# One Strassen step in the gate and up projections of the middle groups of a two-layer decoder trunk

## The chip, the cores and the metric

The kernel runs on one core of a Trainium2 chip. The metric is the device time of one execution in microseconds (us). The engines are named as the profile names them: PE (matrix multiply) and PEld (its weight loads), DVE (vector), ACT (scalar), POOL (GpSimd) and SP, which issues the transfers from HBM.

## What is computed

Two layers; in each a half-step SwiGLU feed-forward block (FFN), a token mixer and a second FFN, with an RMSNorm before and behind each. So there are four FFNs. The change touches the FFNs alone.

```python
D_MODEL = 1024
SEQ = 512
D_FF = 2816
...
def _swiglu(x, wg, wu, wd):
    return (jax.nn.silu(x @ wg) * (x @ wu)) @ wd
...
    for l in range(DEPTH):
        g = norm_g[l]
        h = _swiglu(_rmsnorm(x, g[0]), ffn_w_gate[l, 0], ffn_w_up[l, 0], ffn_w_down[l, 0])
        x = x + 0.5 * _rmsnorm(h, g[1])
```

Inputs and outputs are float32.

## The kernel before

**Numbers.** A float32 operand is held as a pair of tiles in the matmul's 32-bit format, the rounded value (`hi`, written by ACT, `split`, L69) and the rest (`lo`, written by DVE, also L69). A product of two such operands is three matmuls (`mm3`, L74 to L76): hi by hi, hi by lo and lo by hi. The normalized input `hT` of an FFN lies in SBUF as such a pair, channels on the partitions: 8 blocks of 128 channels by 512 tokens.

**The FFN.** The 2816 hidden channels are 22 blocks f of 128. For one f, the gate and the up projection take one weight unit of 128x1024 each (`unit`, L90: a load of 512 KB into one of three buffers `raw`, then the split into `whi` and `wlo`), and 8 channel blocks times three matmuls of 512 columns each (`proj`), into one PSUM bank each. `evac` (L208) turns the two banks into the activations: ACT takes silu of the gate, DVE multiplies by the up projection, and the product is split into `ahi` and `alo`.

Two f make a group g; there are 11 groups. `down(g)` multiplies the activations of a group by the two units of the down matrix: the first 512 output columns gather in four PSUM banks `acc` (24 matmuls), the second 512 go through the four banks `mm` (24 matmuls) and DVE adds each of these banks to a tile `ysb` in SBUF (L252). Group 0 has a form of its own (`first_projs`, matmuls of 256 columns, token half by token half, while the input is still being transposed), and so has group 10, at the end. In between the program is `gate_up(g)` and then `down(g - 1)`, for g = 1 to 9.

**Order.** Each engine works through its own list of instructions in order. The lists are made when the program is built: a scheduler places the instructions, and each instruction carries the semaphore waits that its operands ask for. PSUM holds four rotating banks `mm` and four `acc`. SP issues one load after the other; a load waits until its `raw` buffer is free.

Of the kernel before, what the change touches and what calls it, by code (L numbers as in the profile page):

```python
# [40 lines left out]
class Kernel:  # L41
# [41 lines left out]
    def unit(self, src, inner, pool=None, eng=None):  # L83
# [8 lines left out]
        return [z.rearrange("p (k c) -> p k c", c=inner) for z in (hi, lo)]  # L92

    def proj(self, out, u, toks=slice(0, S), m=P):

        for k in range(KD):
            last = self.mm3(out, [z[:, k, :m] for z in u], [z[:, k, toks] for z in self.hT], k == 0, k == KD - 1)
        return last
# [5 lines left out]

    def first_projs(self, srcs, pooled=3, pool=None):

        units = []
        for n, s in enumerate(srcs):
            units.append(self.unit(s, P, pool, self.nc.gpsimd if n < pooled else None))
            if self.begin:  # L110
                self.guard = self.turned
# [85 lines left out]
    def ffn(self, l, s, norms, nxt, held=None):  # L197
        nc, tc, a = self.nc, self.tc, self.a
        wg, wu, wd = (a[w][l, s] for w in ("ffn_w_gate", "ffn_w_up", "ffn_w_down"))
        with ExitStack() as ctx:  # L200
            self.ring = self.pool("ring", 6, ctx)
            dring = self.pool("dring", 4, ctx, side="right" if l % 2 and s else "left")
            act, yp = self.pool("act", 6, ctx), self.pool("yp", 1, ctx)
            gains = self.pool("gains", 1, ctx)
            ysb = [yp.tile([P, 512], F32, name=f"ysb{t}") for t in range(NT)]
# [12 lines left out]
            def gate_up(g):  # L218
                fs = (2 * g, 2 * g + 1)
                if g == 0:  # L220
                    pg0, pu0, pg1, pu1 = self.first_projs([wg[0], wu[0], wg[1], wu[1]],
                                                          0 if held else 3, dring if s else None)
                    evac(0, pg0, pu0)
                    evac(1, pg1, pu1)
                    return
                for f in fs:
                    evac(f, self.proj_new(wg[f]), self.proj_new(wu[f]))

# [39 lines left out]
            last = [(f, self.unit(wg[f], P), self.unit(wu[f], P)) for f in (NF - 2, NF - 1)]  # L268
            load_down(ng - 2)
# [678 lines left out]
```

## Time and profile before

| | |
|---|---|
| time, median of 3 runs (range) | 1953.24 us (1952.72 to 1953.73) |
| profiled execution: its own time | 1956.74 us |
| profiled execution: its span, first to last instruction | 1955.0 us |
| granted TensorE clock, mean over the span | 0.993 of full speed |
| PE busy | 1918.8 us (98%) |
| PEld, DVE, ACT, POOL busy | 83%, 48%, 37%, 9% |

The span is what the profile's rows add up to; the execution's own time is 1.7 us more. The profiled execution lies 3.5 us (0.2%) over the median of the timed runs.

### The profile page before, as it was taken

Reading aid. Unit: us, or ns where it says so; the run is one execution under the profiler, and the core shown is the slowest. Engines: PE = TensorE matmul, PEld = TensorE weight load, DVE = VectorE, ACT = ScalarE, POOL = GpSimd, SP = SyncE. Lnnn points to the kernel's source line nnn. Section 1 sums busy time; section 2 is a strip of 40 time slices with the busy share of each in tenths; the row PEclk is TensorE's granted clock in tenths of the full one; section 3 lists DMA queues with packets and bytes.
Section 4 is the critical chain, followed back from the end, with each engine's and each line's share of the span. In section 5 each row is a group of like instructions: output and inputs, shape, how many; then the busy total and the mean of one; then the engine's idle time right before and its main releaser. Section 6 shows DMA issues by size and latency. Waiting matters only on the chain.

```text
span 1955.0 us, 24019 instructions
## 1 busy us (share of the span) xinstructions
PE 1918.8 (98%) x9715; PEld 1631.1 (83%) x9715; DVE 939.9 (48%) x1356; ACT 722.6 (37%) x1244; POOL 185.6 (9%) x250
## 2 busy tenths in 40 slices
PE   9999999999999999999999999999999989999998
PEld 8888888987788888888988888898888888888887
DVE  5333333589665333333634343356667563333333
ACT  6322221434764222222532222236666553222221
POOL 1000000332230000000200000014331210000000
PEclk9999999999999999999999999999999999999999
DMA  5423232131034232321342323222212323232311
GB/s 193 130 86 108 86 129 75 45 99 65 22 98 150 85 101 92 102 91 49 120 139 86 108 86 108 65 77 66 65 55 65 108 76 129 87 107 87 107 54 44
DMA packets 51265, 178.39 MB, mean 91 GB/s; under 512 B 7346, under 2 KB 7346, under 8 KB 51154
## 3 DMA queue, kind: packets, MB, share of 16 engines
q1 hardware_dynamic: 51154, 176.86, 28.0%
q8 instruction: 76, 1.25, 0.3%
q14 instruction: 35, 0.29, 0.0%
HBM read 174.74 MB, written 2.10 MB: 90 GB/s over the span
## 4 chain that ended last, share of the span: by engine, by line
PE 52%; issue 39%; DVE 3%; ACT 3%; POOL 2%; DMA 1%; POOLq 0%; DVEq 0%; SPq 0%; ACTq 0%
PE mm L74 14%; PE mm L75 14%; PE mm L76 14%; PE acc L74 2%; PE acc L75 2%; PE acc L76 2%; ACT whi L69 1%; PE mm L708 1%; DVE yv L381 1%; POOL rstd L136 1%; PE mm L718 1%; ACT junk L141 1%; POOL ms L134 1%; DMA raw<-in_ffn_w_up_dram 0%; POOL wlo L69 0%
## 5 line engine op out<-in xcount | busy, mean ns | idle before, releaser
L74 PE MATMUL mm<-hhi,whi 128*128 128x512 f32 (+1 forms) x1952 | 696.1, 359 | 8.7 <-ACT hhi L69 8.3
L75 PE MATMUL mm<-hlo,whi 128*128 128x512 f32 (+1 forms) x1952 | 697.9, 358 | 1.8 <-DVE hlo L69 1.6
L76 PE MATMUL mm<-hhi,wlo 128*128 128x512 f32 (+1 forms) x1952 | 697.3, 358 | 0.0
L69 ACT CAST whi<-raw 128x1024 fp32r<-128x1024 f32 x319 | 330.9, 1050 | 901.0 <-issue 264.0
L69 DVE TENSOR_TENSOR wlo<-raw,whi 128x1024 fp32r<-128x1024 f32 (+1 forms) x293 | 353.9, 1222 | 370.1 <-ACT whi L69 355.8
L74 PEld LDWEIGHTS mm<-hhi,whi 128*128 128x128 f32 x1952 | 370.5, 191 | 63.5 <-ACT hhi L69 10.2
L75 PEld LDWEIGHTS mm<-hlo,whi 128*128 128x128 f32 x1952 | 371.8, 191 | 54.9 <-DVE hlo L69 3.0
L76 PEld LDWEIGHTS mm<-hhi,wlo 128*128 128x128 f32 x1952 | 371.8, 190 | 52.1
L215 DVE TENSOR_TENSOR wk<-mm,wk 128x512 f32<-128x512 f32 (+1 forms) x96 | 62.1, 647 | 290.6 <-PE mm L76 245.2
L252 DVE TENSOR_TENSOR ysb<-mm,ysb 128x512 f32<-128x512 f32 x128 | 88.5, 692 | 161.3 <-PE mm L76 161.3
L134 POOL TENSOR_SCALAR ms<-ss 128x1 f32<-128x1 f32 x48 | 23.6, 491 | 1464.5 <-ACT junk L141 1464.4
L76 PE MATMUL mm<-whi,alo 128*128 128x512 f32 x352 | 137.1, 389 | 0.0
L75 PE MATMUL mm<-wlo,ahi 128*128 128x512 f32 x352 | 137.0, 389 | 0.0
L76 PE MATMUL acc<-whi,alo 128*128 128x512 f32 x352 | 136.9, 389 | 0.0
L74 PE MATMUL acc<-whi,ahi 128*128 128x512 f32 x352 | 136.9, 389 | 0.0
L75 PE MATMUL acc<-wlo,ahi 128*128 128x512 f32 x352 | 136.9, 389 | 0.0
L74 PE MATMUL mm<-whi,ahi 128*128 128x512 f32 x352 | 136.8, 390 | 0.0
L214 ACT ACTIVATE wk<-mm 128x512 f32<-128x512 f32 (+1 forms) x96 | 53.2, 555 | 69.6 <-PE mm L76 69.6
L76 PEld LDWEIGHTS mm<-whi,alo 128*128 128x128 f32 x352 | 66.1, 188 | 13.9
L74 PEld LDWEIGHTS acc<-whi,ahi 128*128 128x128 f32 x352 | 66.1, 188 | 13.8
L76 PEld LDWEIGHTS acc<-whi,alo 128*128 128x128 f32 x352 | 66.0, 188 | 13.8
L75 PEld LDWEIGHTS acc<-wlo,ahi 128*128 128x128 f32 x352 | 66.1, 188 | 13.7
(211 smaller groups left out, 1964.5 us busy)
## 6 DMA issues: line engine op xcount, KB each, us to landing
raw<-in_ffn_w_gate_dram SPq DMA_DIRECT2D x88, 512.0 KB, 3.4
raw<-in_ffn_w_up_dram SPq DMA_DIRECT2D x88, 512.0 KB, 3.9
raw<-in_ffn_w_down_dram SPq DMA_DIRECT2D x88, 512.0 KB, 3.4
raw<-in_fox_w_qk_dram SPq DMA_DIRECT2D x16, 512.0 KB, 3.5
raw<-in_ab_w_in_dram SPq DMA_DIRECT2D x14, 512.0 KB, 3.4
raw<-in_ab_w_out_dram SPq DMA_DIRECT2D x8, 512.0 KB, 3.4
raw<-in_fox_w_out_dram SPq DMA_DIRECT2D x8, 512.0 KB, 3.5
gpost<-in_norm_g_dram SPq DMA_DIRECT2D x6, 512.0 KB, 3.9
```

The lines of the kernel that those rows point to most:

```text
L69: return nc.scalar.copy(hi, src), (eng or nc.vector).tensor_tensor(lo, src, hi.bitcast(F32), ALU.subtract)
L74: mm(out, a[0], b[0], start=start, stop=False)
L75: mm(out, a[0], b[1], start=False, stop=False)
L76: return mm(out, a[1], b[0], start=False, stop=stop)
L134: nc.gpsimd.tensor_scalar(ms, ss[:, 0:1], ss[:, 1:2], eps, ALU.add, ALU.add)
L136: nc.gpsimd.tensor_tensor(r, ms, self.mhalf, ALU.pow)
L141: return self.nc.scalar.activation(junk, src, AF.Square, scale=scale, accum_out=out)
L214: nc.scalar.activation(sg, pg, AF.Silu)
L215: nc.vector.tensor_tensor(av, pu, sg, ALU.mult)
L252: nc.vector.tensor_tensor(ysb[t], p, ysb[t], ALU.add)
L381: nc.vector.scalar_tensor_tensor(yv[c], av[c][:, k : k + S], cw[:, c, k : k + 1], yv[c], ALU.mult, ALU.add)
L708: nc.tensor.transpose(pt[:, c0 : c0 + P], pr[b][:, kb * P : (kb + 1) * P], self.ident)
```

## The change

For f = 2 to 19 (the groups 1 to 9) gate and up are computed together by one Strassen step (in Winograd's form), three matmuls per product as before. The 2x2 blocks of the weight matrix are gate/up by channel halves: `a11`, `a12` are the two channel halves of the gate's unit, `a21`, `a22` those of the up unit (128x512 each). The 2x2 blocks `B` of the input are channel halves by token halves (four blocks of 128 channels by 256 tokens). Seven block products `m1` to `m7`, each four channel blocks times three matmuls of 256 columns, stand for the eight of the plain form: 84 matmuls of 256 columns for 48 of 512. For this

- `combine` makes, once for each FFN, the four sums of input blocks `T[1]` to `T[4]` on DVE, and splits them;
- `winograd(f)` makes four sums of weight blocks on DVE (`s1`, `s2`, and both again), splits seven pieces of 128x512 (`phi`, `plo`) where there were two units of 128x1024, and puts the products together with seven DVE additions of 256 columns out of PSUM, one ACT copy, silu and one multiplication. `m1` and `m5` share a bank, so do `m7` and `m6`, and `m2` and `m3`; the order on PE is m1, m5, m7, m6, m2, m4 and m3.

`down(0)` now stands ahead of `gate_up(1)`; the pools are cut anew (ring 10 halves for 6 units, `act` 4 for 6, the gains' tiles after the sums of the input are given up).

```diff
-            self.ring = self.pool("ring", 6, ctx)
+            self.ring = self.pool("ring", 10, ctx)
...
-                    evac(f, self.proj_new(wg[f]), self.proj_new(wu[f]))
+                    winograd(f)
...
+            halves = slice(0, 256), slice(256, 512)
+            B = {(r, c): [z[:, 4 * r : 4 * r + 4, halves[c]] for z in self.hT] for r in (0, 1) for c in (0, 1)}
+            T = {}
+
+            def combine():
...
+                for ks in (slice(0, 2), slice(2, 4)):
+                    b = {n: [z[:, ks, :].bitcast(F32) for z in w] for n, w in B.items()}
+                    t = {n: self.wk().rearrange("p (k c) -> p k c", c=256) for n in T}
+                    for n, p, m in ((1, (0, 0), (0, 1)), (3, (1, 1), (0, 1))):
+                        v.tensor_tensor(t[n], b[p][0], b[m][0], ALU.subtract)
+                        v.tensor_tensor(t[n], t[n], b[p][1], ALU.add)
+                        v.tensor_tensor(t[n], t[n], b[m][1], ALU.subtract)
+                    for n, p, m in ((2, 1, (1, 1)), (4, 2, (1, 0))):
+                        v.scalar_tensor_tensor(t[n], t[p], -1.0, b[m][0], ALU.mult, ALU.subtract)
+                        v.tensor_tensor(t[n], t[n], b[m][1], ALU.subtract)
+                    for n in (1, 3, 2, 4):
+                        self.split(*[z[:, ks, :] for z in T[n]], t[n])
+
+            def winograd(f):
+                rg, ru = self.load(wg[f]), self.load(wu[f])
+                a11, a12, a21, a22 = (r[:, n * 512 : n * 512 + 512] for r in (rg, ru) for n in range(2))
+                add = lambda o, x, y: nc.vector.tensor_tensor(o, x, y, ALU.add)
+                left, right = halves
+                banks = [self.psum() for _ in range(4)]
+                m1, m7, m2, m4 = (p[:, left] for p in banks)
+                m5, m6, m3 = (p[:, right] for p in banks[:3])
+
+                def product(out, w, b):
+                    for k in range(4):
+                        self.mm3(out, [z[:, k, :] for z in w], [z[:, k, :] for z in b], k == 0, k == 3)
+
+                w1, w2, sg, s1, s2 = (self.wk() for _ in range(5))
+                product(m1, self.piece(a11), B[0, 0])
+                nc.scalar.copy(w1[:, left], m1)
+                add(s1, a21, a22)
+                product(m5, self.piece(s1), T[1])
+                add(s2, s1, a11)
+                add(s1, a11, a21)
+                product(m7, self.piece(s1), T[3])
+                product(m6, self.piece(s2), T[2])
+                add(w1[:, right], m6, w1[:, left])
+                add(w2[:, left], m7, w1[:, right])
+                add(w2[:, right], m5, w2[:, left])
+                add(w1[:, right], m5, w1[:, right])
+                add(s2, s2, a12)
+                product(m2, self.piece(a12), B[1, 0])
+                add(w1[:, left], m2, w1[:, left])
+                product(m3, self.piece(s2), B[1, 1])
+                add(w1[:, right], m3, w1[:, right])
+                nc.scalar.activation(sg, w1, AF.Silu)
+                product(m4, self.piece(a22), T[4])
+                add(w2[:, left], m4, w2[:, left])
+                nc.vector.scalar_tensor_tensor(w2, sg, -1.0, w2, ALU.mult, ALU.mult)
+                aT[f] = [act.tile([P, S], F32R, name=n) for n in ("ahi", "alo")]
+                self.split(*aT[f], w2)
...
-            for g in range(1, ng - 1):
+            combine()
+            down(0, True)
+            gate_up(1)
+            for g in range(2, ng - 1):
                 gate_up(g)
-                down(g - 1, g == 1)
+                down(g - 1, False)
```

Three places of the instruction lists show what this does to the order. In the rows, a name's number is a buffer's; `raw`, `phi`, `plo`, `whi`, `wlo` are as above, and `wk` are work tiles.

**DVE over one middle group, before.** The list from the last addition of a `down` to the last split of the next group's activations (L215 is the multiplication in `evac`):

```order
L252 TENSOR_TENSOR ysb3_202<-mm_1316,ysb3_202 128x512
L69 TENSOR_TENSOR wlo_1675<-raw_1672,whi_1674 128x1024
L69 TENSOR_TENSOR wlo_1681<-raw_1678,whi_1680 128x1024
L69 TENSOR_TENSOR wlo_1606<-raw_1603,whi_1605 128x1024
L215 TENSOR_TENSOR wk_1389<-mm_1355,wk_1388 128x512
L69 TENSOR_TENSOR wlo_1637<-raw_1634,whi_1636 128x1024
L69 TENSOR_TENSOR alo_1387<-wk_1389,ahi_1386 128x512
L69 TENSOR_TENSOR wlo_1744<-raw_1741,whi_1743 128x1024
L215 TENSOR_TENSOR wk_1459<-mm_1425,wk_1458 128x512
L69 TENSOR_TENSOR wlo_1775<-raw_1772,whi_1774 128x1024
L69 TENSOR_TENSOR alo_1457<-wk_1459,ahi_1456 128x512
```

The weight units that are split here are used later: `wlo_1675` and `wlo_1681` are for the `down` of this group.

**First place: DVE and PE behind a `down`, after.** The list of DVE from the last additions of a `down` into the first f of the next group (L335 is the addition to `ysb`, L277 `add`; `wk_1633` is `s1`, `wk_1634` is `s2`):

```order
L335 TENSOR_TENSOR ysb2_198<-mm_1606,ysb2_198 128x512
L69 TENSOR_TENSOR alo_1551<-wk_1420,ahi_1550 128x512
L335 TENSOR_TENSOR ysb3_199<-mm_1614,ysb3_199 128x512
L277 TENSOR_TENSOR wk_1633<-raw_1624 128x512
L277 TENSOR_TENSOR wk_1634<-wk_1633,raw_1622 128x512
L69 TENSOR_TENSOR plo_1654<-wk_1633,phi_1653 128x512
L277 TENSOR_TENSOR wk_1633<-raw_1622,raw_1624 128x512
L69 TENSOR_TENSOR plo_1672<-wk_1633,phi_1671 128x512
L69 TENSOR_TENSOR plo_1688<-wk_1634,phi_1687 128x512
L69 TENSOR_TENSOR plo_1709<-raw_1622,phi_1708 128x512
L277 TENSOR_TENSOR wk_1634<-wk_1634,raw_1622 128x512
```

PE has, behind the last matmul of that `down` (into `mm_1614`), the twelve of m1, whose last three stand here, and then m5 and m7 (`mm_1627`), which read the pieces of `s1`:

```order
L74 MATMUL mm_1626<-hhi_118,phi_1635 128x256
L75 MATMUL mm_1626<-hlo_119,phi_1635 128x256
L76 MATMUL mm_1626<-hhi_118,plo_1636 128x256
L74 MATMUL mm_1626<-t1hi_504,phi_1653 128x256
L75 MATMUL mm_1626<-t1lo_505,phi_1653 128x256
L76 MATMUL mm_1626<-t1hi_504,plo_1654 128x256
```

The piece of `s1` is now made behind the last addition of the `down`, and its first user stands twelve matmuls behind that `down` on PE. On ACT the copy of m1 (L289) stands ahead of the cast `phi_1653`.

**Second place: DVE between the two f of a group, after.** From the addition of m4 of the first f to the first pieces of the second (`wlo_1911` and `wlo_1917` are the units of the down matrix, L308 is the last multiplication of `winograd`):

```order
L277 TENSOR_TENSOR wk_1631<-mm_1629,wk_1631 128x256
L69 TENSOR_TENSOR wlo_1911<-raw_1908,whi_1910 128x1024
L277 TENSOR_TENSOR wk_1630<-mm_1628,wk_1630 128x256
L277 TENSOR_TENSOR wk_1776<-raw_1767 128x512
L308 SCALAR_TENSOR_TENSOR wk_1631<-wk_1632,wk_1631 128x512
L277 TENSOR_TENSOR wk_1777<-wk_1776,raw_1765 128x512
L69 TENSOR_TENSOR plo_1797<-wk_1776,phi_1796 128x512
L69 TENSOR_TENSOR alo_1762<-wk_1631,ahi_1761 128x512
L277 TENSOR_TENSOR wk_1776<-raw_1765,raw_1767 128x512
L69 TENSOR_TENSOR wlo_1917<-raw_1914,whi_1916 128x1024
L69 TENSOR_TENSOR plo_1815<-wk_1776,phi_1814 128x512
```

The load of `raw_1908` waits for the buffer of `raw_1624` (the up unit of the first f), whose last reader is the split of `a22`, `plo_1744`; that of `raw_1914` waits for `wlo_1911`. PE has between m3 of the first f and m5 of the second twelve matmuls of `down`, which read `whi_1910` and `wlo_1911`.

**Third place: DVE at the start of the first FFN.** Before, from the first multiplication of group 0:

```order
L215 TENSOR_TENSOR wk_474<-mm_224,wk_473 128x512
L69 TENSOR_TENSOR wlo_593<-raw_590,whi_592 128x1024
L69 TENSOR_TENSOR wlo_631<-raw_628,whi_630 128x1024
L69 TENSOR_TENSOR alo_472<-wk_474,ahi_471 128x512
L69 TENSOR_TENSOR wlo_637<-raw_634,whi_636 128x1024
L215 TENSOR_TENSOR wk_482<-mm_226,wk_481 128x512
L69 TENSOR_TENSOR wlo_704<-raw_701,whi_703 128x1024
```

And after, from the same multiplication (L231) into the sums of the input (L265 to L270):

```order
L231 TENSOR_TENSOR wk_487<-mm_237,wk_486 128x512
L69 TENSOR_TENSOR alo_485<-wk_487,ahi_484 128x512
L231 TENSOR_TENSOR wk_495<-mm_239,wk_494 128x512
L265 TENSOR_TENSOR wk_512<-hhi_118 128x512
L265 TENSOR_TENSOR wk_513<-hhi_118 128x512
L266 TENSOR_TENSOR wk_512<-wk_512,hlo_119 128x512
L69 TENSOR_TENSOR alo_493<-wk_495,ahi_492 128x512
L266 TENSOR_TENSOR wk_513<-wk_513,hlo_119 128x512
```

The sums stand behind the multiplication that waits for the last bank of group 0 (`mm_239`). From there to the piece of the first `s1` there are 31 instructions of 128x512 on DVE, while PE has the 48 matmuls of `down(0)` and the twelve of the first m1.

## Rows read from the trace of the kernel before

**Rows 1.** The page: busy us and share of the span of each engine

```profile
PE 1918.8 (98%) x9715; PEld 1631.1 (83%) x9715; DVE 939.9 (48%) x1356; ACT 722.6 (37%) x1244; POOL 185.6 (9%) x250
```

**Rows 2.** Busy time by engine in one middle group (windows), with granted clock

```profile
233.33:265.97 32.64, 32.64 (x145) 27.03 (x144) 12.43 (x15) 8.38 (x10) 0.00 (x0) 1.00 0.30 98
```

**Rows 3.** Timeline of DVE in that group: start, us, instruction, idle before

```profile
233.33 0.69 DVE L252 TENSOR_TENSOR ysb<-mm,ysb 128x512 f32<-128x512 f32 x1 [2.93 <-PE mm L76]
...
237.41 0.69 DVE L252 TENSOR_TENSOR ysb<-mm,ysb 128x512 f32<-128x512 f32 x1 [0.67 <-PE mm L76]
238.02 1.22 DVE L69 TENSOR_TENSOR wlo<-raw,whi 128x1024 fp32r<-128x1024 f32 x1
...
249.85 0.69 DVE L215 TENSOR_TENSOR wk<-mm,wk 128x512 f32<-128x512 f32 x1 [3.57 <-PE mm L76]
...
265.97 0.69 DVE L252 TENSOR_TENSOR ysb<-mm,ysb 128x512 f32<-128x512 f32 x1 [2.93 <-PE mm L76]
```

**Rows 4.** Timeline of ACT in that group, the split behind DVE's L215

```profile
250.57 0.62 ACT L69 CAST ahi<-wk 128x512 fp32r<-128x512 f32 x1 [0.28 <-DVE wk L215]
```

**Rows 5.** Timeline, all engines: matmuls of 512 columns, and DVE behind one

```profile
300.90 0.39 PE L76 MATMUL mm<-whi,alo 128*128 128x512 f32 x1
...
301.33 0.69 DVE L252 TENSOR_TENSOR ysb<-mm,ysb 128x512 f32<-128x512 f32 x1 [0.67 <-PE mm L76]
...
303.62 0.39 PE L74 MATMUL mm<-hhi,whi 128*128 128x512 f32 x1
...
304.30 0.39 PE L74 MATMUL mm<-hhi,whi 128*128 128x512 f32 x1
```

**Rows 6.** Timeline of PE in group 0: matmuls of 256 columns

```profile
24.01 0.28 PE L74 MATMUL mm<-hhi,whi 128*128 128x256 f32 x1
...
24.36 0.28 PE L74 MATMUL mm<-hhi,whi 128*128 128x256 f32 x1
```

**Rows 7.** Groups by line and shape: count, busy us, mean ns, idle before

```profile
L69 DVE TENSOR_TENSOR wlo<-raw,whi 128x1024 fp32r<-128x1024 f32 x290 | 351.3, 1225 | 369.0 <-ACT whi L69 354.7 <-PE mm L76 4.7
L69 ACT CAST whi<-raw 128x1024 fp32r<-128x1024 f32 x316 | 328.6, 1052 | 898.6 <-issue 264.0 <-PE mm L76 254.4 <-DMA raw<-in_ffn_w_down_dram 179.8
L69 DVE TENSOR_TENSOR alo<-wk,ahi 128x512 fp32r<-128x512 f32 x80 | 54.8, 685 | 2.7 <-ACT ahi L69 2.7
L69 ACT CAST ahi<-wk 128x512 fp32r<-128x512 f32 x80 | 49.6, 621 | 23.3 <-DVE wk L215 23.3
L156 DVE SCALAR_TENSOR_TENSOR x<-wk,rstd,x 128x512 f32<-128x512 f32 x48 | 33.9, 747 | 3.5 <-POOL rstd L136 3.1
L173 ACT ACTIVATE wk<-wk,rstd 128x512 f32<-128x512 f32 x24 | 17.3, 720 | 10.2 <-POOL rstd L136 9.9
L215 DVE TENSOR_TENSOR wk<-mm,wk 128x256 f32<-128x256 f32 x16 | 6.8, 425 | 44.7 <-ACT wk L214 44.7
L214 ACT ACTIVATE wk<-mm 128x256 f32<-128x256 f32 x16 | 6.1, 381 | 51.5 <-PE mm L76 51.5
```

**Rows 8.** Timeline of DVE at the end of an FFN

```profile
354.57 0.69 DVE L295 TENSOR_TENSOR ysb<-mm,ysb 128x512 f32<-128x512 f32 x1 [4.80 <-PE mm L76]
355.30 0.69 DVE L152 TENSOR_TENSOR wk<-ysb,gpost 128x512 f32<-128x512 f32 x1
```

**Rows 9.** DMA issues: count, KB each, median us from issue to landing

```profile
raw<-in_ffn_w_down_dram SPq DMA_DIRECT2D x88, 512.0 KB, 3.4
```

**Rows 10.** Timeline of PE in a mixer: matmuls behind two waits

```profile
496.76 0.44 PE L472 MATMUL mm<-ident,z 128*128 128x128 f32 x2 [2.77 <-ACT z L464]
...
531.68 0.50 PE L74 MATMUL mm<-whi,chi 128*128 128x512 f32 x1 [1.69 <-ACT chi L69]
532.01 0.40 PE L75 MATMUL mm<-wlo,chi 128*128 128x512 f32 x1
```

**Rows 11.** The same windows view around the first of these waits

```profile
495.00:500.00 5.00, 3.24 (x13) 2.76 (x13) 5.00 (x12) 3.52 (x12) 0.03 (x1) 0.71 0.00 0
```

More of the change, by code (lines that the diff above doesn't have):

```diff
@@ L92, in unit, with piece, pieces @@
         return [z.rearrange("p (k c) -> p k c", c=inner) for z in (hi, lo)]
+    def piece(self, src, eng=None):
+        pair = [self.ring.tile([P, 512], F32R, name=n) for n in ("phi", "plo")]
+        with ExitStack() as after:
+            for ins in self.guard:
+                after.enter_context(self.tc.issue_after(ins.ins))
+            self.split(*pair, src, eng)
+        return [z.rearrange("p (k c) -> p k c", c=P) for z in pair]
+    def pieces(self, src, eng=None):
+        raw = self.loaded.pop(0) if self.loaded else self.load(src)
+        return tuple(self.piece(raw[:, n * 512 : n * 512 + 512], eng) for n in range(2))
     def proj(self, out, u, toks=slice(0, S), m=P):
         for k in range(KD):
-            last = self.mm3(out, [z[:, k, :m] for z in u], [z[:, k, toks] for z in self.hT], k == 0, k == KD - 1)
+            w = [z[:, k % 4, :] for z in u[k // 4]] if isinstance(u, tuple) else [z[:, k, :m] for z in u]
+            last = self.mm3(out, w, [z[:, k, toks] for z in self.hT], k == 0, k == KD - 1)
         return last
@@ L103, in proj_new, with first_projs @@
         return out
-    def first_projs(self, srcs, pooled=3, pool=None):
+    def first_projs(self, srcs, pooled=3, pool=None, pieces=False):
         units = []
         for n, s in enumerate(srcs):
-            units.append(self.unit(s, P, pool, self.nc.gpsimd if n < pooled else None))
+            eng = self.nc.gpsimd if n < pooled else None
+            units.append(self.pieces(s, eng) if pieces else self.unit(s, P, pool, eng))
             if self.begin:
@@ L221, in gate_up @@
                     pg0, pu0, pg1, pu1 = self.first_projs([wg[0], wu[0], wg[1], wu[1]],
-                                                          0 if held else 3, dring if s else None)
+                                                          0 if held else 3, dring, not s)
                     evac(0, pg0, pu0)
@@ L259, in ffn @@
                 held.close()
-            for g in range(1, ng - 1):
+            combine()
+            down(0, True)
+            gate_up(1)
+            for g in range(2, ng - 1):
                 gate_up(g)
-                down(g - 1, g == 1)
+                down(g - 1, False)
+            combos.close()
+            gains = self.pool("gains", 1, ctx)
             with tc.issue_after(self.loading.ins) if held else ExitStack():
@@ L267, in ffn @@
                 gpre = self.load_gain(gains, *nxt, "gpre") if nxt else None
-            last = [(f, self.unit(wg[f], P), self.unit(wu[f], P)) for f in (NF - 2, NF - 1)]
+            last = [(f, self.pieces(wg[f]), self.pieces(wu[f])) for f in (NF - 2, NF - 1)]
             load_down(ng - 2)
```

8 lines of the change are left out of this document (6 added, 2 removed).

## The prediction

> **What bounds the kernel now.** The page comes first: PE is busy for 98% of the span, DVE for 48%, ACT for 37% [rows 1]. A busy PE need not be a PE at its peak, so the next view is the windows of one middle group: PE busy in all 32.64 us of it, at the full clock, DVE in 12.43, ACT in 8.38 [rows 2]. The timeline of DVE then shows the period: the first addition of a `down` comes at 233.33 and 265.97 us, 32.64 us apart [rows 3]. A group is 144 matmuls of 512 columns; 32.64/144 is 0.2267 us each, and three successive ones stand 0.68 us apart on the timeline [rows 5]. So PE never waits in the middle groups: DVE and ACT split weights that are needed later, and the kernel goes as fast as matmuls follow each other. The reader is to see two things here: only fewer or shorter matmuls can help, and the slack of DVE (20 us in a group) is what the change spends.
>
> **What PE saves.** In `first_projs` three matmuls of 256 columns take 0.35 to 0.36 us [rows 6]; I take 0.12 each. Two of them (0.24) cost more than one of 512 (0.2267), so of the eighth that the step saves in columns little over half is left: for one f, 48 x 0.2267 = 10.88 us become 84 x 0.12 = 10.08, a gain of 0.80 us. The eighteen f of an FFN give 14.4 us, the four FFNs 57.6. A group would go from 32.64 to 168 x 0.12 + 48 x 0.2267 = 31.04 us.
> The Trainium skill (TensorE: Matmul & The Clock Gate, Back-to-back issue gap) gives a gap of N/2.4 + 2.5 ns, that is 109 and 216 ns, and by it the gain would be 48 x 0.2158 - 84 x 0.1092 = 1.19 us for one f and 85 us in all. The rows show 120 and 227, so this page is too good for both shapes, and the sum goes by the rows.
>
> **What DVE gets.** For one f DVE had two units of 1.225 us, one multiplication and one split; now it has seven pieces and four weight sums (0.69 each), seven additions of 256 columns (0.425), the last multiplication (0.75) and a split (0.69) [rows 7]. With two down units and four additions, a group comes to 14 x 0.69 + 8 x 0.69 + 14 x 0.425 + 2 x 0.75 + 2 x 0.69 + 2 x 1.225 + 4 x 0.69 = 29.2 us of 31.04. Instructions that don't depend on each other overlap by 0.08 us (237.41 to 238.02 for one of 0.69 us [rows 3]), which brings it near 26. DVE is thus not the bound in sum. But it is now early enough only where its order lets it run ahead, and at four kinds of joint the order does not. The prices for a hand-over: DVE starts 0.43 us after the start of the last matmul it needs (300.90 to 301.33 [rows 5]), that is 0.20 behind PE's issue; an instruction that needs the one before it starts 0.04 after its end [rows 8]; ACT starts 0.03 after DVE (249.85 + 0.69 to 250.57 [rows 3, 4]), and I take as much from ACT to DVE and 0.05 to PE; a cast of 512 takes 0.62, silu from SBUF 0.72 (as L173), a copy of 256 columns out of PSUM 0.38 [rows 7]; the first matmul behind a wait costs PE 0.1 more (0.33 us to the next for 0.23 [rows 10]).
>
> **Joint A, behind a `down` (first place of the change's lists).** Time 0 is where PE has issued the last matmul of the `down`. The last `ysb` addition runs from 0.20 to 0.89, `s1` from 0.81 to 1.50. PE issues m1 until 1.44, ACT copies it from 1.64 to 2.02 and only then casts `s1`, until 2.6; `plo` of `s1` is ready at 3.32. The third matmul of m5 needs it: 3.35 where 1.68 would have been free, 1.7 us lost. `s1` is then overwritten (its reader was that split): 3.35 to 4.04, cast until 4.7, split until 5.4. The third matmul of m7 starts at 5.45, where 4.9 was free, 0.55 lost. With two restarts 2.4 us. The lower bound leaves out the copy and the restarts: 1.85. This joint stands ahead of the groups 3 to 9, seven times in an FFN.
>
> **Joint B, between the f of a group (second place).** The load of the first down unit waits for the split of `a22`, which by the same count ends at 9.6; 3.4 us to landing [rows 9] makes 13.1, the cast (1.05) 14.2, the split (1.22) 15.4. PE, 2.4 us late, reaches the `down` at 13.9 and waits 0.3 for the cast and 0.3 for the split. Behind that split DVE does the addition of m3 (to 15.8); silu ends at 16.55, the last multiplication at 17.3, `s2` at 17.9, the piece of `s1` at 18.6. PE, through its twelve matmuls at about 17.2, wants it at 17.45: 1.1 us. The second unit costs another 0.1. I take 1.8; if the first unit lands in time, the chain from m3 alone leaves 0.4, and with a slower load it is 2.5. Eight times in an FFN.
>
> **Joint P, from f = 2 to 3 and from 3 to 4.** Here no `down` lies between m3 and the next m5. Addition of m3, silu, multiplication, `s2` and the split end 3.35 us behind m3, where 0.24 was free; m7 then loses 1.0 as in joint A. With restarts 4.4 us, at least 3.2, twice in an FFN.
>
> **Joint S, the start (third place).** The sums of the input begin with the multiplication that ends group 0, 0.8 us behind its last matmul. 31 instructions at 0.60 to 0.75, mean 0.61, take 18.9: the first piece of `s1` is ready at 19.7. PE has 48 x 0.2267 + 1.44 = 12.3 us of work: the third matmul of m5 comes 7.2 us late, and m7 another 1.0: 8.4 us with restarts, at least 6.5 (DVE's list alone). `down(0)` itself is covered: its activations are split while the last two banks of group 0 are filled.
>
> **Costed at nothing.** The moved `down(0)` takes its two loads and splits along; they land and are split during the 46 matmuls of 256 columns of group 0 that PE still has by then (5.5 us). The two loads of gains now wait for the last product that reads the sums `T`, and SP has four loads of the down matrix behind them: some 3.4 us each [rows 9], and PE does not want the first of the four until 18 matmuls of the last full `down` and 96 of the half projections are through (4.1 + 11.5 us). Were this cover gone, the two loads would cost up to 7 us in each FFN. The two mixers keep their lists of instructions.
>
> **Sum.** Per FFN 7 x 2.4 + 8 x 1.8 + 2 x 4.4 + 8.4 = 48.4 us lost against 14.4 gained: 34 us, 136 for four. The clock adds a little: behind a wait of 2.77 us the granted clock was 0.71 in the five microseconds from 495 [rows 10, 11], 2.4 GHz for part of them and 1.2 for the rest. Joints P and S wait as long, twelve in all. At half clock PE loses up to 1.6 us for each, part of which it would have waited anyhow; I put 6 us for all twelve, between 0 and 20. 1956.7 + 142 = 2099 us for a profiled execution. The timed runs lay 3.5 below it: **2095 us**, 7% slower. I see nothing that hides the joints: PE's own list is in order, and what stands behind the late product waits with it.
>
> Bounds: with A at 1.85, B at 0.4, P at 3.2 and S at 6.5 an FFN loses 29 - 14.4 = 14.7 us, and the time is 2012. With B at 2.5 and the clock also falling at the 28 joints A (1.2 us each), 136 + 22 + 34 + 6 makes 2151.
>
> **Rivals.**
> 1. *Faster.* If DVE and ACT ran ahead as before, the 57.6 us would remain: 1896; with joint S alone (34 us) 1930. It decides at 14.4 us of waits in an FFN: joint A alone, seven times, brings 13 to 17. For it speaks that DVE's sum fits into a group; against it, that the last `ysb` addition waits for PE and `s1` stands behind it on the same engine. Chance 0.06.
> 2. *Joints partly hidden*, 1960 to 2040: loads land earlier and the waits of B vanish, prices at their lower bounds. Speaks for it: a group has 5 us of DVE to spare. Chance 0.16.
> 3. *The clock falls at joint A too*, 2125 to 2170. Two short waits in a row might do it, though the single one of 1.69 us at 530 us left matmuls at their full rate behind it [rows 10]. Chance 0.14.
> 4. *No change*, within 0.2% (the bound that a measurement of this kernel can tell): only if gains and joints cancel, between rivals 1 and 2. Chance 0.02.
>
> The forecast itself (2040 to 2125) has 0.62. The range 2015 to 2150 leaves out rivals 1 and 4, half of 2's lower part and the upper end of 3, together two in ten. Faster by over 0.2%: 0.06; same 0.02; slower 0.92.
>
> **What would show it.** Right: successive groups 34.5 to 35.5 us apart at the last `ysb` addition; PE waits on L74 and L76 for `phi` and `plo`, about 2 us behind each `down`; `acc` matmuls waiting for `whi` and its DMA; one wait of 5 to 7 us early in each FFN; DVE near 75% in the groups, PE under 90%. Wrong: groups at 31 to 32 us, or 256-column matmuls not 0.12 us apart. I would be wrong above all if DVE's list were not what holds `s1` back, or if ACT and DVE hand over faster than the rows here show.

## The result, and the profile after

The changed kernel takes **2100.39 us** (median of 4 executions, 2099.53 to 2101.0) and the kernel before 1952.98 us (median of 4, 1952.21 to 1953.73): a ratio of 1.0754, 95% interval 1.0736 to 1.0773, so it is 7.5% slower. The forecast was 2095 us, range 2015 to 2150. The profiled execution took 2099.85 us with a span of 2098.1 us, 143.1 us over the span of before. One of the four executions of e5 (below) took 3055.82 us at a mean granted clock of 0.557, and the numbers given for e5 leave it out.

The page of the changed kernel, busy us and share of the span by engine, answers to [rows 1]:

```profile
PE 1947.0 (93%) x12307; PEld 1737.5 (83%) x12307; DVE 1514.6 (72%) x2641; ACT 907.0 (43%) x1732; POOL 187.2 (9%) x253
```

The windows of one middle group, from the last `ysb` addition of one `down` to that of the next (us, then busy us and count of PE, PEld, DVE, ACT and POOL, granted clock, DMA share, GB/s), answer to [rows 2]:

```profile
227.80:262.86 35.06, 32.91 (x218) 29.43 (x217) 26.70 (x47) 12.96 (x22) 0.00 (x0) 1.00 0.30 91
```

A group is 35.06 us now, 2.42 longer than before, at the full clock, and PE is no longer busy in all of it. The 28 such periods of the four FFNs are 34.7 to 37.5 us, 35.2 on average. DVE works 26.70 us in a group, where 12.43 were needed before.

Where the time of a group goes is read from the timeline. First joint A. DVE, ACT and PE behind the same `down`:

```profile
227.80 0.69 DVE L335 TENSOR_TENSOR ysb<-mm,ysb 128x512 f32<-128x512 f32 x1
228.41 0.68 DVE L277 TENSOR_TENSOR wk<-raw 128x512 f32<-128x512 f32 x1
...
230.15 0.69 DVE L69 TENSOR_TENSOR plo<-wk,phi 128x512 fp32r<-128x512 f32 x1 [0.33 <-ACT phi L69]
```

```profile
229.23 0.37 ACT L289 COPY wk<-mm 128x256 f32<-128x256 f32 x1 [3.01 <-PE mm L76]
229.50 0.62 ACT L69 CAST phi<-wk 128x512 fp32r<-128x512 f32 x1
```

```profile
228.91 0.28 PE L76 MATMUL mm<-hhi,plo 128*128 128x256 f32 x1
230.17 0.38 PE L74 MATMUL mm<-t1hi,phi 128*128 128x256 f32 x1 [0.98 <-ACT phi L69]
230.40 0.28 PE L75 MATMUL mm<-t1lo,phi 128*128 128x256 f32 x1
230.90 0.39 PE L76 MATMUL mm<-t1hi,plo 128*128 128x256 f32 x1 [0.22 <-DVE plo L69]
...
233.00 0.39 PE L76 MATMUL mm<-t3hi,plo 128*128 128x256 f32 x1 [0.22 <-DVE plo L69]
```

The reader is to see the chain in the order of the forecast: the last `ysb` addition, s1, ACT's copy of m1, the cast, the split; and PE, through m1 at 228.91, waiting for the cast and then for the split. A wait costs more than the idle time in brackets: from 228.91 to 230.17 it is 1.26 us where 0.12 would do, and the matmul behind a wait takes 0.23 to the next. Over all steps of this joint that is 1.73 us at m5 and 0.68 at m7. Joint B of the same group adds 0.45 us at the `down` matmuls (waits for `whi` and `wlo`), 0.92 at m5, which waits for `plo`, and 0.22 behind:

```profile
242.74 0.50 PE L75 MATMUL acc<-wlo,ahi 128*128 128x512 f32 x1
...
245.74 0.39 PE L76 MATMUL mm<-t1hi,plo 128*128 128x256 f32 x1 [0.66 <-DVE plo L69]
```

Then the start of the first FFN, joint S, and the first joint P (timeline of PE):

```profile
56.72 0.58 PE L74 MATMUL mm<-t1hi,phi 128*128 128x256 f32 x1 [5.42 <-ACT phi L69]
...
58.48 0.58 PE L76 MATMUL mm<-t1hi,plo 128*128 128x256 f32 x1 [0.96 <-DVE plo L69]
...
59.29 0.41 PE L76 MATMUL mm<-t1hi,plo 128*128 128x256 f32 x1
59.50 0.41 PE L74 MATMUL mm<-t1hi,phi 128*128 128x256 f32 x1
...
72.77 0.39 PE L74 MATMUL mm<-t1hi,phi 128*128 128x256 f32 x1 [2.02 <-ACT phi L69]
...
73.92 0.58 PE L76 MATMUL mm<-t1hi,plo 128*128 128x256 f32 x1 [0.65 <-DVE plo L69]
```

and the windows view around joint S:

```profile
53.20:63.40 10.20, 5.72 (x25) 5.43 (x26) 8.93 (x15) 4.34 (x9) 0.00 (x0) 0.50 0.00 0
```

During the wait of 5.42 us the granted clock falls to 0.50, and until 63.4 us successive matmuls stand 0.21 us apart (59.29 to 59.50) where 0.12 is the step in the groups. At this joint P the clock falls too, at 73.7 us, in the shorter wait behind that of 2.02 us; at the second joint P of this FFN it falls within the wait of 2.02 us itself, at 87.3.

### The profile page after: what moved, and what is told of

Same layout as the page of the kernel before. It is cut to its first block, busy times and chain, and to the rows that moved or that the text cites. A ratio compares the mean times of both kernels' runs of the same rounds, so it can differ in the third digit from the quotient of the medians.

```text
span 2098.1 us, 31167 instructions
## 1 busy us (share of the span) xinstructions
PE 1947.0 (93%) x12307; PEld 1737.5 (83%) x12307; DVE 1514.6 (72%) x2641; ACT 907.0 (43%) x1732; POOL 187.2 (9%) x253
## 4 chain that ended last, share of the span: by engine, by line
PE 49%; issue 23%; DVE 15%; ACT 7%; DMA 5%; POOL 1%; ACTq 0%; POOLq 0%; DVEq 0%; SPq 0%
PE mm L76 14%; PE mm L74 14%; PE mm L75 13%; DVE plo L69 5%; DMA raw<-in_ffn_w_down_dram 4%; DVE wk L277 3%; ACT phi L69 2%; ACT whi L69 2%; PE acc L74 2%; PE acc L75 2%; PE acc L76 2%; DVE wk L308 1%; ACT wk L305 1%; PE mm L796 1%; DVE yv L469 1%
## 5 line engine op out<-in xcount | busy, mean ns | idle before, releaser
L74 PE MATMUL mm<-hhi,phi 128*128 128x256 f32 x1248 | 352.1, 283 | 1.9 <-ACT hhi L69 1.3
L75 PE MATMUL mm<-hlo,phi 128*128 128x256 f32 x1248 | 353.2, 283 | 0.1
L76 PE MATMUL mm<-hhi,plo 128*128 128x256 f32 x1248 | 352.4, 283 | 0.0
L69 DVE TENSOR_TENSOR plo<-wk,phi 128x512 fp32r<-128x512 f32 x288 | 192.4, 689 | 90.1 <-ACT phi L69 89.9
L74 PEld LDWEIGHTS mm<-hhi,phi 128*128 128x128 f32 x1248 | 238.7, 192 | 7.5 <-ACT hhi L69 2.1
L75 PEld LDWEIGHTS mm<-hlo,phi 128*128 128x128 f32 x1248 | 239.1, 192 | 4.5 <-DVE hlo L69 0.5
L277 DVE TENSOR_TENSOR wk<-mm,wk 128x256 f32<-128x256 f32 x504 | 193.6, 420 | 66.8 <-PE mm L76 64.2
L69 DVE TENSOR_TENSOR wlo<-raw,whi 128x1024 fp32r<-128x1024 f32 (+1 forms) x128 | 156.5, 1229 | 116.7 <-ACT whi L69 114.2
L76 PEld LDWEIGHTS mm<-hhi,plo 128*128 128x128 f32 x1248 | 238.9, 191 | 0.0
L69 DVE TENSOR_TENSOR plo<-raw,phi 128x512 fp32r<-128x512 f32 x258 | 172.4, 689 | 6.7 <-ACT phi L69 6.5
L69 ACT CAST phi<-raw 128x512 fp32r<-128x512 f32 x264 | 154.0, 617 | 19.2 <-DMA raw<-in_ffn_w_up_dram 10.3
```

The costliest lines, as they stand in the source:

```text
L69: return nc.scalar.copy(hi, src), (eng or nc.vector).tensor_tensor(lo, src, hi.bitcast(F32), ALU.subtract)
L74: mm(out, a[0], b[0], start=start, stop=False)
L75: mm(out, a[0], b[1], start=False, stop=False)
L76: return mm(out, a[1], b[0], start=False, stop=stop)
L277: add = lambda o, x, y: nc.vector.tensor_tensor(o, x, y, ALU.add)
```

## The experiments

The times are of single executions, unless an interval is given; the kernel before took 1952.0 to 1955.0 beside them. Where the text says groups, it means the 28 periods from one last `ysb` addition to the next.

### The lists: whose tiles, and one copy

**e1.** The sums leave the rotating work tiles.

```diff
-            self.ring = self.pool("ring", 10, ctx)
+            self.ring = self.pool("ring", 8, ctx)
+            sums = self.pool("sums", 4, ctx)
...
-                w1, w2, sg, s1, s2 = (self.wk() for _ in range(5))
+                w1, w2, sg = (self.wk() for _ in range(3))
+                s1, s2 = (sums.tile([P, 512], F32, name="sum") for _ in range(2))
```

> The two weight sums of winograd get a pool of their own (4 buffers; ring 8 halves instead of 10) in place of work tiles. DVE's work stays the same; in its list the sum s1 of the next f now stands ahead of the ysb additions and of the additions of the f before, not behind them. Theory (the hand-overs at the joints, set by the order of DVE's list): joint A falls from the 2.4 us measured to 0.4 or less, joint B from 1.6 to 0.6, joint P from 3.3 and more to about 1, the start stays; per FFN 14 + 8 + 5 = 27 us less, 108 in all: about 1990 us (1970 to 2030), groups near 32.3 us apart. Rival 1 (DVE's amount of work is the bound, 26 to 29 us of a 31 us group): groups stay at 34.5 or more, 2080 to 2105 us. Rival 2 (the loads, through three raw buffers, hold the joints): the loads are as before, the time stays above 2070.

Measured: **1943.05 us**, 0.6% under the kernel before beside it (1954.71), one execution of each. The windows view of a middle group of e1:

```profile
235.55:266.63 31.08, 31.08 (x217) 29.17 (x216) 26.22 (x46) 13.24 (x22) 0.00 (x0) 1.00 0.30 103
```

PE is busy in all of the group again, and the group is 31.08 us, the 31.04 of the forecast without any wait. DVE has the same work as in the changed kernel (26.22 us). So the amount of DVE's work doesn't bound, and the loads don't either: rivals 1 and 2 fall. Joint B went altogether, which is more than expected.

**e9** is the counterpart, and **e7** the control for the smaller ring.

```diff
-                w1, w2, sg, s1, s2 = (self.wk() for _ in range(5))
+                w1, w2, sg = (outs.tile([P, 512], F32, name="out") for _ in range(3))
+                s1, s2 = (self.wk() for _ in range(2))
```

> The counterpart of e1: the sums s1 and s2 stay among the work tiles, and the other three tiles of winograd (w1, w2, sg) get a pool of their own (5 buffers; ring 8). In DVE's list the sums then stand ahead of the last ysb addition as in e1. Theory (the five tiles of one f rotate through seven work buffers in the order of the program, so the sums of the next f are placed behind the activation of this one): as e1, groups at 31.1 to 32, 1945 to 1970 us. Rival (the sums must have a pool of their own, or e1's gain has another cause): 2050 or more.

> The changed kernel with the ring cut from 10 to 8 halves and nothing else, as a control for e1: in the first FFN DVE's list stays the same row for row. Theory: 2100 us (2093 to 2110). If the smaller ring were what made e1 fast: under 2000.

Measured: e9 **1946.59 us**, groups 31.08; e7 **2118.36 us**, groups 35.2, above the expected 2093 to 2110. It is enough that the sums and the other three tiles don't come out of one pool, whichever moves. The smaller ring is no gain by itself; why it costs 18 us was not followed up. Both e1 and e9 also raise the number of work buffers, from seven to eleven and to twelve; one pool with as many was not tried, so the separation isn't told from the number.

**e12.** One line moved, no pool changed:

```diff
                 product(m1, self.piece(a11), B[0, 0])
-                nc.scalar.copy(w1[:, left], m1)
                 add(s1, a21, a22)
...
                 product(m6, self.piece(s2), T[2])
+                nc.scalar.copy(w1[:, left], m1)
                 add(w1[:, right], m6, w1[:, left])
```

DVE's list at joint A then reads (`wk_1987` is s1, `wk_1988` is s2):

```
L277 TENSOR_TENSOR wk_1987<-raw_1978 128x512
L308 SCALAR_TENSOR_TENSOR wk_1774<-wk_1775,wk_1774 128x512
L277 TENSOR_TENSOR wk_1988<-wk_1987,raw_1976 128x512
L335 TENSOR_TENSOR ysb1_197<-mm_1952,ysb1_197 128x512
L69 TENSOR_TENSOR plo_2007<-wk_1987,phi_2006 128x512
L335 TENSOR_TENSOR ysb2_198<-mm_1960,ysb2_198 128x512
L69 TENSOR_TENSOR alo_1905<-wk_1774,ahi_1904 128x512
L277 TENSOR_TENSOR wk_1987<-raw_1976,raw_1978 128x512
L335 TENSOR_TENSOR ysb3_199<-mm_1968,ysb3_199 128x512
```

> The changed kernel with one line moved: ACT's copy of m1 stands in the program behind the product m6 instead of behind m1. Tiles, pools and the amount of work are the same, PE's list of the FFNs too. In DVE's list of joint A s1, s2, the piece of s1 and the second s1 now stand ahead of the last ysb addition; at joint B, at the joints P and at the start the list is as it was. Theory (the place of s1 in the lists makes joint A): joint A's 2.4 us go, seven times in an FFN, and nothing else changes: groups at 32.5 to 33 us in place of 35.1, 67 us less in all, 2033 us (2010 to 2050). Rival (the sums need a pool of their own, or joint A has another cause): groups at 34.5 or more, 2085 to 2110 us.

Measured: **2041.02 us**, a group of e12 in the windows:

```profile
224.47:257.10 32.63, 31.93 (x218) 29.30 (x218) 26.25 (x47) 12.84 (x22) 0.00 (x0) 1.00 0.28 97
```

Most groups are 32.5 to 33 us. In the group shown PE's steps have no excess at joint A, and 1.4 us of it at joint B. This prices joint A alone: 2.4 us, as put down. The total came out 8 us higher than expected, as much as the clock takes: over all matmuls in stretches at 0.50, the steps are 39.2 us longer than at the full clock in e12, and 30.8 us in the changed kernel.

### The amount of work on DVE

**e10** takes the four sums of an f off DVE, in work tiles as in the changed kernel.

```diff
+                wsum = lambda o, x, y: nc.gpsimd.tensor_tensor(o, x, y, ALU.add)
...
-                add(s1, a21, a22)
+                wsum(s1, a21, a22)
```

The other three sums change in the same way.

> The four weight sums of an f are made on GpSimd instead of DVE, in the work tiles as before; DVE has 5.5 us less to do in a group. s1 no longer stands behind the ysb addition, but its piece plo still does, and at joint B the list now has the split wlo of the second down unit ahead of that piece. Theory (the lists): joint A falls from 2.4 to about 1.2, joint B grows from 1.6 to 3 or 4, since the piece waits behind a split that waits for a load: groups at 35 to 37 us, about 2125 us (2085 to 2165). Rival 1 (DVE's amount of work is the bound): groups at 31.5 to 33, 1990 to 2040 us.

Measured: **2156.75 us**, most groups 36.4 to 36.7. A group in the windows:

```profile
271.56:308.30 36.74, 33.67 (x218) 29.39 (x217) 21.60 (x39) 12.89 (x22) 11.41 (x8) 1.00 0.24 87
```

DVE has 5.1 us less to do (21.60), and the group is 1.7 us longer. The time is in the expected range, but the joints were not as expected: joint A took 3.1 us (1.7 at m5 as before, 1.4 at m7), joint B 2.4. The timelines of GpSimd and ACT of e10 show why m5 gained nothing:

```profile
262.91 1.30 POOL L278 TENSOR_TENSOR wk<-raw 128x512 f32<-128x512 f32 x1 [3.29 <-DMA raw<-in_ffn_w_up_dram]
```

```profile
272.99 0.37 ACT L290 COPY wk<-mm 128x256 f32<-128x256 f32 x1 [3.01 <-PE mm L76]
273.26 0.62 ACT L69 CAST phi<-wk 128x512 fp32r<-128x512 f32 x1
```

s1 is ready at 264.21, and its cast starts at 273.26: it stands behind the copy of m1 in ACT's list, and the copy waits for PE. So the copy on ACT holds m5 at joint A by itself, even with s1 nine microseconds early. m7 loses more than before because its sum takes 1.29 us on GpSimd (274.75 to 276.04) where DVE took 0.69: this part of e10's price is not the lists.

At the start of each FFN GpSimd and DVE get in each other's way:

```profile
48.53 8.81 POOL L278 TENSOR_TENSOR wk<-raw 128x512 f32<-128x512 f32 x1 [28.13 <-DVE t2lo L69]
```

```profile
55.54 0.68 DVE L270 TENSOR_TENSOR wk<-wk,hlo 128x512 f32<-128x512 f32 x1
58.02 1.22 DVE L69 TENSOR_TENSOR plo<-wk,phi 128x512 fp32r<-128x512 f32 x1 [1.80 <-ACT phi L69]
```

The first s1 takes 8.81 us (GpSimd's spans are rough in a profile), about as long as DVE's sums of the input go on beside it, and PE's wait at joint S is 7.14 us in place of 5.42. The split at 58.02, beside the next GpSimd addition, takes 1.22 us where 0.69 is usual. All three are the same in the four FFNs.
The Trainium skill (Perfetto Trace Analysis, Optimizing Scalar/DVE Operations) warns that GpSimd and DVE share a read port to SBUF, so that moving work from one to the other may not help. The rows at the start of the FFNs agree with it. At joint A of the group shown it isn't the reason: the second s1 takes 1.29 us and the splits 0.69, as they do alone.

**e11** is e6 (below) with more work on DVE, whose results nobody reads:

```diff
                 self.split(*aT[f], w2)
+                add(w1, w1, w1)
+                add(sg, sg, sg)
```

> e6 with two more additions of 128x512 on DVE for each f behind its activation, whose results nobody reads: DVE is busy for 28.6 us of a group of 31.08 instead of 26.2. Theory (the lists, not the amount): PE still has no wait in the groups, 31.1 to 31.6 us apart, 1904 to 1920 us. Rival 1 (the amount of DVE's work sets the time, and e6 won by chance of its order): 2.4 us more in each of 28 periods, 1955 to 1975 us.

Measured: **1906.76 us** (e6: 1904.03); a group of e11:

```profile
259.39:290.49 31.10, 31.10 (x218) 29.13 (x218) 27.81 (x51) 12.84 (x22) 0.00 (x0) 1.00 0.29 102
```

Another 1.6 us on DVE cost 0.02 in this group. Less work on DVE made the kernel slower (e10), more left it as fast (e11).

### Buffers, and another order of the products

**e2.** The down units get load buffers of their own.

```diff
-            self.ring = self.pool("ring", 10, ctx)
+            self.ring = self.pool("ring", 8, ctx)
+            more = self.pool("more", 2, ctx)
...
-                    wdu[f] = self.unit(wd[f], D, dring)
+                    raw = more.tile([P, 1024], F32, name="raw")
+                    wdu[f] = self.unit(wd[f], D, dring, raw=raw)
```

> The down units get two load buffers of their own (ring 8 halves instead of 10), so that their loads wait for no split of gate or up. In DVE's list the two splits wlo of the down units move forward, to right behind the last ysb addition of the group before, one ahead of s1 and one ahead of its piece. Theory (order of DVE's list): the waits of the down matmuls for whi and wlo (0.45 us in a group) vanish, but s1 and its piece come later by up to 2 x 1.2 us less the cast that they hide: joint A grows from 2.4 to about 3.9, groups to 36 to 37 us, about 2130 us (2105 to 2165), slower than the changed kernel. Rival 2 (the loads hold the joints): joint B falls from 1.6 to under 0.4, 2040 to 2065 us. Rival 1 (amount of DVE's work): 2095 to 2105.

Measured: **2157.82 us**, groups 35.2 to 37.6. The timeline of DVE of e2 behind a `down`:

```profile
200.25 0.69 DVE L337 TENSOR_TENSOR ysb<-mm,ysb 128x512 f32<-128x512 f32 x1 [0.27 <-PE mm L76]
200.86 1.22 DVE L69 TENSOR_TENSOR wlo<-raw,whi 128x1024 fp32r<-128x1024 f32 x1
...
202.60 0.68 DVE L278 TENSOR_TENSOR wk<-raw 128x512 f32<-128x512 f32 x1
203.20 1.22 DVE L69 TENSOR_TENSOR wlo<-raw,whi 128x1024 fp32r<-128x1024 f32 x1
```

The splits stand around s1, as expected, and the time is in the expected range, but not for that reason. PE's list has changed too. Behind m1 it now has the `acc` matmuls of the next `down`, which cover a part of joint A: its excess is 2.0 us there. None are left between m3 and the next m5, so joint B has become a joint P, with a wait of 2.02 us for `phi` in every group. Where the clock stays up, a group is about as long as in the changed kernel; in 20 of the 28 it falls to 0.50 for a stretch behind that wait, and those take 36.7 to 37.6 us. One of each kind in the windows:

```profile
165.04:200.25 35.21, 32.43 (x218) 29.41 (x217) 25.80 (x45) 12.29 (x22) 0.00 (x0) 1.00 0.26 91
200.25:237.51 37.26, 33.87 (x218) 30.50 (x217) 27.09 (x47) 13.32 (x24) 0.00 (x0) 0.95 0.24 85
```

So of the 57 us that e2 is slower, some 37 are matmuls at half clock, by their steps (68.0 us in all, 30.8 in the changed kernel). PE's waits for `phi` are 115 us in all, 66 in the changed kernel.

**e4 and e8.** In `winograd` the products with raw pieces come first, m1, m2, m4, m5, m7, m6, m3 in the program; e8 adds the two buffers of e2.

```diff
                 add(s1, a21, a22)
+                add(s2, s1, a11)
+                product(m2, self.piece(a12), B[1, 0])
+                product(m4, self.piece(a22), T[4])
                 product(m5, self.piece(s1), T[1])
-                add(s2, s1, a11)
                 add(s1, a11, a21)
                 product(m7, self.piece(s1), T[3])
...
-                product(m2, self.piece(a12), B[1, 0])
...
-                product(m4, self.piece(a22), T[4])
```

> The same seven products in another order of the program: m1, m2 and m4, which read pieces of the raw weights, then m5, m7, m6 and m3, which read pieces of sums. DVE's work and the place of s1 behind the last ysb addition stay; PE has 36 matmuls of 256 columns (4.3 us) ahead of the first product with a sum in place of 12 (1.4 us), and the raw buffers come free earlier. Theory (hand-overs at the joints): the chain of 3.3 us behind a down is covered, joint A falls from 2.4 to 0.2 or less, B from 1.6 to 0.2 or less (the raw buffer of the up unit is free earlier), P from 3.3 to under 0.5, the start from 7.2 by 2.9; per FFN 15 + 11 + 6 + 3 = 35 us less, 140 in all: about 1960 us (1935 to 1995), groups at 31.1 to 31.6. Rival 1 (DVE's amount of work): groups at 33 or more, above 2020.

Measured: **2129.24 us**, 134 us above the expected range: a clear miss. PE's waits in e4 (total us, times, longest):

```profile
PE acc L74 <- ACT whi L69: 75.7, 32, 2.9
PE mm L74 <- DVE wk L277: 56.3, 40, 2.6
PE mm L74 <- ACT phi L69: 16.6, 13, 3.3
```

The waits for pieces are nearly gone, as expected. But the `down` matmuls now wait for `whi`, and other matmuls for the additions out of PSUM that free a bank. In 17 of the 28 groups the clock falls behind such a wait; those take 36.3 to 39.6 us, the others 34.8 to 35.8. By the steps, matmuls at half clock make 23 of the 29 us that e4 is slower than the changed kernel. The time also fits rival 1, but what PE waits for in these rows, and e1 and e11, speak against DVE's amount of work.

> e4 (m1, m2, m4 ahead of the products with sums) with the two load buffers of e2. In e4 the waits for the pieces had gone, and waits of the down matmuls for whi (2.3 to 2.4 us in a group, 76 us in all) and of matmuls for PSUM banks (56 us) stood in their place. Theory (s1 stands behind the last ysb addition and delays PE by two routes, the piece that m5 reads and the raw buffer that the next down unit's load waits for): with both routes covered the groups fall to 31.5 to 33.5, about 1990 us (1960 to 2035). Rival 1 (DVE's amount of work, or the banks): groups stay above 34.5, 2080 or more.

Measured: **2075.43 us**, groups 34.60, again outside what was expected and near the rival (the banks). The waits for `whi` have gone; what is left, and large, is

```profile
PE mm L74 <- DVE wk L278: 110.5, 72, 2.1
```

1.7 us and 1.6 us in each group. As I read it, a bank that m1 and m5 share, now the first and the fourth product, stays taken until additions that stand late in DVE's list; this was not tried by itself. My expectations covered m5, and covering it alone passed the delay on, to the load and then to the banks.

### The start, and a version that is faster than both

**e3.** Group 1 in the plain form, the rest as in the changed kernel.

```diff
+            def plain(f):
+                out = [self.psum() for _ in range(2)]
+                for o, w in zip(out, (wg, wu)):
+                    self.proj(o, self.pieces(w[f]))
+                evac(f, *out)
...
                 for f in fs:
-                    winograd(f)
+                    if g == 1:
+                        plain(f)
+                    else:
+                        winograd(f)
```

> Group 1 goes back to the plain form (four pieces of 128x512 for its two units, 512 columns), the Strassen step is kept for the groups 2 to 9; the 31 instructions of combine then lie beside down(0) and the 96 matmuls of group 1 (10.9 + 21.8 us). Theory: the wait at the start (5.6 + 1.3 + 0.3 us) goes, of the two joints P one is left (f = 3 to 4, sums behind the activation of f = 3), 1.6 us of gain are lost: about 10 us less in an FFN, 40 in all, and the half-clock stretches at the start of the FFNs (some 20 us in each) shrink to a third, worth another 10 to 20: about 2045 us (2025 to 2065); the groups 3 to 9 stay 35.1 us apart. Rival (the start is hidden elsewhere or moves to the next joint): 2080 to 2100.

Measured: **2077.61 us**, short of the expected 2025 to 2065. The start gave what was expected: the last `ysb` addition of the first group moves from 121.78 to 107.74 us, 14 us. But the groups became 36.2 us long: PE's waits for `whi` grew from 4.8 us (5 times) to 25.6 (53 times). From the last `ysb` addition to the cast of `whi` it is 13.95 us there (216.28 to 230.23) and 12.58 in the changed kernel (227.80 to 240.38); 0.4 of it is an addition that DVE's list now has ahead of the split of a22, the rest stays open.

**e5 and e6** put the edits of e1 and e3 together; e6 keeps the plain form for f = 2 alone:

```diff
-                    if g == 1:
+                    if f == 2:
                         plain(f)
```

> Sums in a pool of their own (as in e1) and group 1 in the plain form (as in e3). Theory (hand-overs set by the lists): the groups 3 to 9 stay at the 31.08 us of e1, 1.56 us under the kernel before, seven times in an FFN; the start loses its waits for the sums of the input (7 us measured in e1) and gives 1.6 us of gain back, so that the first ysb addition comes at about 105.5 us, 1.3 ahead of the kernel before: 12.2 us per FFN, 49 in all: 1905 us (1895 to 1925). Rival (the start's waits move to the first Strassen group, as they partly did in e3): 1925 to 1945.

> As e5, but only f = 2 in the plain form: combine (some 19 us of DVE) then has the 48 matmuls of down(0) and the 48 of f = 2 beside it (21.8 us). Theory: if that is cover enough, 0.8 us per FFN better than e5, 3 in all: 1902 us (1893 to 1915). Rival: the last sums of the input come late, waits of 2 us and a stretch at half clock in each FFN: 1912 to 1930, slower than e5.

Measured: e5 **1925.08 us** (median of three), ratio to the kernel before 0.9855 (0.9835 to 0.9875); e6 **1904.03 us**, ratio **0.9753** (0.9739 to 0.9768). e5 came out 20 us over the expected time, and not in its rival's way: nothing waits at the start, but most of its groups are 31.4 to 32.4 us long. Why its lists are worse than those of e6 stays open. The page and a group of e6:

```profile
PE 1863.4 (98%) x12163; PEld 1698.7 (89%) x12163; DVE 1466.8 (77%) x2585; ACT 907.0 (48%) x1716; POOL 188.1 (10%) x253
```

```profile
257.69:288.77 31.08, 31.08 (x217) 29.16 (x216) 26.23 (x47) 12.99 (x22) 0.00 (x0) 1.00 0.33 109
```

PE saves 1.56 us in a group against [rows 2]. Seventeen f at the forecast's 0.80 us make 54 us in four FFNs; the profiled executions differ by 1956.74 - 1904.42 = 52.3. The Strassen step gives what the matmul steps promise once nothing waits.

## Why the prediction was right, step by step

**What PE saves: right.** Matmuls of 256 columns stand 0.12 us apart in the changed kernel and groups without waits are 31.08 us (e1, e6). By the gap that the Trainium skill gives (TensorE: Matmul & The Clock Gate, Back-to-back issue gap) a group would have gained an estimated 2.4 us. The rows say 1.56, and the measurement decides.

**The joints: right in kind and place, close in size.** Us per FFN, put down and measured:

| term | put down | measured |
|---|---|---|
| A, seven times | 16.8 (2.4 each) | 16.8 (2.40 each) |
| B, eight times | 14.4 (1.8 each) | 12.6 (1.58 each) |
| P, twice | 8.8 (4.4 each) | 6.2 (3.1 each) |
| S, once | 8.4 | 7.1 |
| half clock | 1.5 (6 in all) | 6.8, 7.0, 3.8, 7.9 |
| gain | -14.4 | -14.4 |

The measured prices are the steps between matmuls over 0.12 (or 0.2267) us, in the group shown for A and B and at the start of the first FFN for P and S; the clock is given for each of the four FFNs. The term that was mis-sized is the clock: 25.5 us instead of 6, outside the 0 to 20 that was allowed for it. (The forecast's 1.6 us for each wait has no working; rows 11 would give 5.00 x 0.29 = 1.45.) It is what the matmuls in the stretches at 0.50 take longer than at the full clock, 0.213 us from one to the next instead of 0.12, restarts included. In return the waits of m7 behind P and S, put down as 1.0 each, mostly don't appear: while PE goes through m5 at half speed, the second piece gets ready. At the one joint P where the clock stayed up (1087.65 us, third FFN) m7 does wait, for 0.40 and 0.23 us. The clock is 19.5 us over what was put down, and B, P and S are 23 under it in the four FFNs; that the total is right to 1 us is luck.

The sum per FFN was 34 and the last additions to `x` (L156 before, L172 after) show for the four FFNs 32.7, 33.5, 34.0 and 40.1 us more than before, and 2.7 more for the two mixers (2.0 less and 4.7 more): 143.0 us for 142 forecast.

The measured column adds up to 35.1 for the first FFN, 2.4 more than it lost. In the profile of the changed kernel group 0 ends 2.6 us earlier: `down(0)` starts at 38.79 us there, and before it would have started at 63.13 - 96 x 0.2267 = 41.37. The first matmuls before stand 0.21 us apart until 19.2 us; those of the changed kernel stand 0.12 apart almost from the start. The forecast has no term for this, and one profile of each doesn't show whether it belongs to the change. The 40.1 us of the fourth FFN contain two waits of `acc` matmuls for `whi`, 1.95 us (1780.33) and 1.00 (2030.48), that the others don't have; what is left of its excess stays open.

**What holds s1 back: half right.** The forecast said that it is DVE's list, with ACT's copy as a link of the chain. e10 shows that the copy is more than a link: with s1 off DVE's list and early, m5 still loses its 1.7 us. The copy waits for PE, which is still in the `down`, and in ACT's list the cast of s1 stands behind it. In the changed kernel both hold. s1 ends at 229.09 us, the copy starts at 229.23 and the cast at 229.50, so without the copy the cast would come some 0.4 us earlier, by an estimate from these rows. e12 moved the copy, and with it s1 came ahead of the `ysb` additions; joint A went, but the run doesn't tell the two apart. What ties s1 to the copy in the list is, as I read e1, e9 and e12, that `w1`, which the copy is the first to write, is taken from the same pool of seven buffers ahead of `s1` (the numbers in the lists are those of tiles, more than there are buffers). That the scheduler hands out the tiles of one pool in the program's order is my reading of three lists, not shown by itself. It is a matter of the lists and not of a buffer that is still taken when the kernel runs: in e10, with the same seven, s1 is written at 262.91, ten microseconds ahead of the copy.

**Costed at nothing: right.** No step of PE at `down(0)` of the first FFN is long until the wait at 56.72. From the last `ysb` addition of the middle groups to the last addition to `x` of the first FFN it is 54.1 us (368.11 to 422.2), and 54.2 before (335.33 to 389.5): the gains' later loads cost nothing. In the other three FFNs it is as long as before or up to 1.1 us shorter.

**The rivals.** Against 1 (faster) and 2 (joints hidden) stand the waits themselves; but e1 shows how near rival 1 was: the same work in two pools is 1943. The clock of rival 3 did not fall at joint A: it is 1.00 over the groups, though two waits of 1.26 and 0.50 us follow each other. Of the signs named, PE under 90% was wrong (93%, since a matmul's record is longer than its step; by the steps it is 31.08 of 35.06 us in the group, 89%), and the waits for `whi` are small.

## What to carry to other kernels

When an edit puts serial work between two engines that had slack, don't compare sums of busy time: write the hand-over chain out at each joint, with every instruction that stands ahead of a link on its own engine. Then ask why the late instruction stands there. Here the answer was a copy that waits for PE and a pool that it shares with the sums, and a move of one line was worth 59 us, while less work on DVE, more buffers or products in a friendlier order moved the delay or made it worse. And count the clock with the waits: most of what e2 and e4 lose against the changed kernel is matmuls at half clock behind waits of 2 us and more.

## What was not expected of the hardware

Waits of the same length can go either way. Behind or within the wait of 2.02 us at joint P the granted clock fell to 0.50 (1.2 GHz) at seven of the eight joints P of the changed kernel and at three of eight in e10, and behind the same wait in 20 of the 28 groups of e2. At the others it stayed at 1.00, and nothing in the rows shown tells them apart. Behind the 0.98 us at joint A, seven times in each FFN, it never fell. A large part of the price of such waits lies behind them: the three of 5.4, 2.0 and 2.0 us at the start of the first FFN brought 6.8 us of slow steps with them.

An addition of 128x512 on GpSimd took 8.81 us instead of 1.3 beside DVE instructions without a gap, at the same place in all four FFNs (e10).
